# Six written-out turns of GpSimd's gather ring, eighteen more waits behind its drain, and list weights made five chunks at a time

## The chip, the cores and the metric

The kernel runs on one core of a Trainium2 chip. The metric is the device time of a run in microseconds, the median of several runs. The profile covers one execution of the program; its span, from the program's first instruction to its last, is a little shorter than the device time.

## What is computed

For each of eight sequences of 8192 rows of 512 numbers, the reference sums all rows up to the midpoint of the sequence's length, and multiplies the sum by a 512x512 matrix:

```
mask = (pos < lengths[:, None, None]).astype(np.float32)
cs = np.cumsum(x * mask, axis=1)
mid_features = cs[b_idx, lengths // 2, :]
return np.matmul(mid_features[:, None, :], w).squeeze(1)
```

Only rows 0 to `lengths // 2` of each sequence matter, so the kernel reads just those and sums them on TensorE.

## The kernel before

**The pieces of x.** Eight consecutive rows of one sequence make a unit of 16 KB. The first 64 rows of all sequences are always read (`xb`, fetched last, in two parts), so are rows 64 to 255 (`xt`, two early loads), and the rest is a list of units that depends on the lengths. The list is cut into chunks of 128 units, one for each partition; there are at most `C` = 31 chunks, and 13 with this draw of lengths. Each chunk is fetched by one indirect DMA of up to 2 MB into one of `R` = 3 buffers.

**The engines.** Each engine runs its own program, and semaphores tie them together.

- VectorE (line 272 on) works out the list of units (`table`) and the weights, zeros and ones that say which rows of a unit count for which sequence (`weights`, line 355). The weights of the first three chunks are made early; those of chunks 3 to 30 by one call at line 371, after a wait for the first two products. A call is two operations, `early` (a comparison) and `wc` (a product). Each step waits for the one before it. The mark `"w"` stands behind the last.
- GpSimd (line 210 on) issues the gathers: three written out at line 236, and the rest by `ring` (line 123), a loop written out for three turns, one for each buffer, which goes round until a register with the number of chunks left is used up. A turn waits on `s_now`, which ScalarE raises when a chunk's unit numbers are in place. After the last chunk (`gp_end`, line 255) GpSimd issues the two parts of `xb` and the pieces of `w`, drains, and waits for the output stores (`s_out`) before it leaves.
- ScalarE (line 165 on) copies, for each chunk, unit numbers to `now` and weights to `ww`; in the ring's first buffer it waits for the mark `"w"` (line 187).
- SyncE (line 134 on) relays: data landed and weights written gives one count of `s_rdy`.
- TensorE (line 393 on) waits for that count and adds eight products of a chunk to `s_ps`. Between chunks it runs idle products[...]. At the end it adds `xb` into `d_ps`, folds both (`mf_ps`), and multiplies by `w` (`o_ps`), waiting for the pieces of `w` by `s_w`.

SyncE and ScalarE use the same `ring`. All transfers of GpSimd go through one queue in the order of issue, so `xb` and `w` come behind the gathers.

Of the kernel before, what the change touches and what calls it, by code (L numbers as in the profile page):

```python
# [15 lines left out]
def kernel(  # L16
# [22 lines left out]
    R = 3  # L39
# [6 lines left out]
    C = -(-B * (S // 2 // U + 1 - HU) // P)  # L46
    FAR = 1 << 17
    IDLE = 2
    xu = x.rearrange("b (q u) d -> (b q) (u d)", u=U)
    lens_words = lengths.tensor.reshape([B]).bitcast(I32).ap().rearrange("(o t) -> o t", o=1)  # L50

# [8 lines left out]
    def sem(name):  # L60
        return tc.alloc_semaphore(name)
# [45 lines left out]
    s_back = [sem(f"back{k}") for k in range(PARTS)]  # L107
    s_w = [sem(f"w{k}") for k in range(4)]
# [11 lines left out]
    def weights_by_rows(at, n):  # L120
        return ww[:, at * B:(at + n) * B].rearrange("p (u b) -> p u b", b=B)

    def ring(eng, name, left, body):
        for s in range(R):
            with nc.body(f"{name}_0_{s}", valid_engines=[eng.engine]):
                eng.br_cmp(left, s, f"{name}_1_{s}", f"{name}_end", "IS_GT")  # L126
            with nc.body(f"{name}_1_{s}", valid_engines=[eng.engine]):
                body(s)
                if s == R - 1:
                    eng.reg_sub(left, left, R)  # L130
                eng.br(f"{name}_0_{(s + 1) % R}")


    def sync(sp):
        left = sp.alloc_register("left_sp")
        full = sp.alloc_register("full_sp")
        have = sp.alloc_register("have_sp")
        sp.reg_mov(full, 16)
        sp.reg_mov(have, 1)
        sp.wait_ge(s_dve, marks["count"])  # L140
        sp.load(left, count[:])
        sp.wait_ge(s_dve, marks["front"])
        sp.wait_ge(s_zero, 3)
        for f in range(PARTS):
            sp.wait_ge(s_front[f], 16)
            sp.sem_inc(s_rdy, 1)
        sp.br("sy_0_0")

        def relay(s):
            sp.wait_ge(s_wr, have)  # L150
            sp.wait_ge(s_full[s], full)
            sp.sem_inc(s_rdy, 1)
            sp.reg_add(have, have, 1)
            if s == R - 1:
                sp.reg_add(full, full, 16)

        ring(sp, "sy", left, relay)
        with nc.body("sy_end", valid_engines=[sp.engine]):
            sp.wait_ge(s_dve, marks["out0"])
            sp.wait_ge(s_act, 3)  # L160
            store(sp, 0)
            sp.br(END)


    def scalar(act):
# [16 lines left out]
        def weigh(s):  # L182
# [7 lines left out]
            act.reg_add(turn, turn, 1)  # L190

        ring(act, "ac", left, weigh)
        with nc.body("ac_end", valid_engines=[act.engine]):
            act.wait_ge(s_pe, 2)
# [15 lines left out]
    def gpsimd(pool):  # L210
        pool.iota(v_i[:], pattern=[[P * U, C], [1, U]], base=HEAD, channel_multiplier=0)
        pool.iota(r_i[:, FU:], pattern=[[2, BU], [-(BU // 2), FB]], base=0,
                  channel_multiplier=BU // 2).then_inc(s_pool, 1)
        pool.wait_ge(s_pool, 1)
        for k in range(4):
            pool.iota(at_i[32 * k:32 * k + 32], pattern=[[P, C]],
                      base=64 * (k % 2) + 8 * (k // 2) + 63 * 8 * k,
                      channel_multiplier=16).then_inc(s_pool, 1)
        pool.tensor_scalar(out=row[:, 2 * B + 2:], in0=lens[:, ::2], scalar1=0.5, scalar2=0.25,
                           op0=ALU.mult, op1=ALU.add)._wait_ge(s_len, 16).then_inc(s_pool, 1)  # L220
        pool.wait_ge(s_pool, 6)
        pool.iota(r_i[:, :FU], pattern=[[2, FU], [-(FU // 2), FB]], base=2 * TOP,
                  channel_multiplier=FU // 2)
        pool.iota(fold_i[:], pattern=[[-32, 2], [-1, B]], base=P, channel_multiplier=1,
                  ).then_inc(s_pool, 1)

        def fetch(to, units, at, n, full):
            return pool.indirect_dma_start(  # L228
                out=to, out_offset=None, in_=units,
                in_offset=bass.IndirectOffsetOnAxis(ap=at, axis=0),  # L230
                bounds_check=n - 1, oob_is_err=False).then_inc(full, 16)

        left = pool.alloc_register("left_pool")
        pool.wait_ge(s_dve, marks["idx"])
        pool.br("gp_b_0")
        for c in range(R):
            if c > 0:
                with nc.body(f"gp_a_{c}", valid_engines=[pool.engine]):
                    pool.br_cmp(left, c, f"gp_b_{c}", "gp_end", "IS_GT")
            with nc.body(f"gp_b_{c}", valid_engines=[pool.engine]):  # L240
                got = fetch(xt[:, c], xu, now[:, c:c + 1], B * UB, s_full[c])
                if c > 0:
                    got._wait_ge(s_done, c)
                if c == 0:
                    pool.load(left, count[:])  # L245
                if c == R - 1:
                    pool.reg_sub(left, left, R)
                pool.br(f"gp_a_{c + 1}" if c + 1 < R else "gp_0_0")

        def gather(s):  # L250
            fetch(xt[:, s], xu, now[:, s:s + 1], B * UB, s_full[s])._wait_ge(s_now, 1)
            pool.sem_inc(s_now, -1)  # L252

        ring(pool, "gp", left, gather)
        with nc.body("gp_end", valid_engines=[pool.engine]):
            for f in range(PARTS):
                pool.dma_start(out=xb[:, f], in_=x[FB * f:FB * (f + 1), :TOP].rearrange(  # L257
                    "b (q u) d -> q b (u d)", u=BU)).then_inc(s_back[f], 16)
            pool.dma_start(out=wt[:, :2], in_=w[HALVES[0]].rearrange("(p k) d -> p k d", k=2),
                           ).then_inc(s_w[0], 16)  # L260
            pool.dma_start(out=wt[:, 2], in_=w[QUARTERS[2]]).then_inc(s_w[1], 16)
            for g, at in enumerate(HALVES):
                pool.dma_start(out=wt[:, 3, at], in_=w[QUARTERS[3], at]).then_inc(s_w[2 + g], 16)  # L263
            pool.drain()
            pool.wait_ge(s_out, 32)
            pool.br(END)

# [4 lines left out]
    def vector(dve):  # L272
        def step(do, *args, wait=True, **kw):
            if done[0] and wait:
                dve.wait_ge(s_dve, done[0])
            do(*args, **kw).then_inc(s_dve, 1)  # L276
            done[0] += 1
# [4 lines left out]
        def mark(name):  # L282
            marks[name] = done[0]
# [30 lines left out]
        def over(t, a, n):  # L314
            return t.unsqueeze(1).to_broadcast((P, a, n))
# [39 lines left out]
        def weights(a, e):  # L355
            n = e - a
            step(tt, out=early[:, a:e].rearrange("p c u b -> p (c u) b"),
                 in0=v_f[:, a * U:e * U].unsqueeze(2).to_broadcast((P, n * U, B)),
                 in1=over(ends[:], n * U, B), op=ALU.is_lt)
            step(tt, out=wc[:, a:e].rearrange("p c (u b) -> p c u b", b=B), in0=early[:, a:e],  # L360
                 in1=ge[:, a:e, :B].unsqueeze(2).to_broadcast((P, n, U, B)), op=ALU.mult)
# [6 lines left out]
        step(ts, out=fold2[:], in0=fold_m[:], scalar1=0, scalar2=None, op0=ALU.is_equal)  # L368
        step(tt, out=fold[:], in0=fold2[:, 0], in1=fold2[:, 1], op=ALU.add)
        dve.wait_ge(s_done, PARTS)  # L370
        weights(R, C)
        mark("w")
        all_done = dve.alloc_register("all_done_dve")
        dve.load(all_done, count[:])
# [18 lines left out]
    def tensor(pe):  # L393
# [5 lines left out]
        def idle(n):  # L399
            for _ in range(n):  # L400
                pe.matmul(idle_ps[:FB], lhsT=ones[:, :FB], rhs=ones[:, :1].to_broadcast((P, D)),  # L401
                          start=True, stop=True, skip_group_check=True)
# [24 lines left out]
        with nc.body("pe_idle", valid_engines=[pe.engine]):  # L427
            idle(IDLE)
            pe.br("pe_to")
# [4 lines left out]
        with nc.body("pe_end", valid_engines=[pe.engine]):  # L434
# [17 lines left out]
            for k in range(KC):  # L452
# [9 lines left out]
            pe.br(END)  # L462

    programs = [(nc.vector, vector, "dv"), (nc.sync, sync, "sy"), (nc.scalar, scalar, "ac"),
                (nc.gpsimd, gpsimd, "gp")]
    for f in range(PARTS):
        nc.sync.dma_start(out=xt[:, f + 1, :FU * D], in_=x[FB * f:FB * (f + 1), TOP:HEAD].rearrange(
            "b (q u) d -> q b (u d)", u=FU)).then_inc(s_front[f], 16)
    nc.scalar.dma_start(out=lens[:], in_=lens_words).then_inc(s_len, 16)
    left = nc.tensor.alloc_register("left_pe")  # L470
# [37 lines left out]
```

## Time and profile before

| what | value |
|---|---|
| device time, median of 3 runs | 83.02 us (82.86 to 83.16) |
| span of the profiled execution | 80.4 us |
| granted TensorE clock | 0.996 |
| bytes moved by DMA | 31.23 MB, 388 GB/s over the span |
| gathers | 13, 0.98 us each on GpSimd (median) |
| `early` and `wc` for chunks 3 to 30 | 2.0 us each on VectorE |
| GpSimd's drain at line 264 | 11.99 us, from 65.6 us |

The page cuts the span into 40 slices of 2 us and gives for each the busy share of every engine, of the DMA engines, and the bytes moved. Busy time of GpSimd is that of its engine; its waits, branches and the drain belong to its sequencer and are listed apart. "Idle before" names what ended an engine's idle time. A chain of waits, followed back from the last instruction, shows what the end waited for.

### The profile page before, as it was taken

The numbers are of one execution on the slowest core, as the hardware profiler recorded it, in microseconds if no ns is written. First come the engines' busy times: TensorE is split into PE (matmuls) and PEld (weight loads), VectorE is DVE, ScalarE is ACT, GpSimd is POOL, SyncE is SP. The second block draws the span as 40 slices with busy tenths as digits, with TensorE's granted clock in tenths as the row PEclk, the third lists the DMA queues.
The fourth block names the chain that finished last, engine by engine and source line by source line (L and its number), as shares of the span: only waits on it lengthen the run. The fifth ranks groups of instructions, "written<-read, shape, count | busy, mean of one in ns | idle before, by whom it ended". The sixth has DMA issues, their size and how long they took to land.

```text
span 80.4 us, 1176 instructions
## 1 busy us (share of the span) xinstructions
PE 59.6 (74%) x360; PEld 14.1 (18%) x360; DVE 11.8 (15%) x43; ACT 9.7 (12%) x31; POOL 19.9 (25%) x32
## 2 busy tenths in 40 slices
PE   0599998997693957939488493975939679399940
PEld 0212212120110202112020110201102021112820
DVE  0799300891000000000000000000000000003130
ACT  2971010102010010201001020010100100000220
POOL 5432050754022040310404004040220793000000
PEclk9999999999999999999999999999999999999998
DMA  0899999999999999999999999999999999999700
GB/s 0 299 428 434 442 418 432 432 424 448 399 456 416 432 432 432 440 399 448 432 415 448 432 424 416 432 448 399 448 432 424 416 432 448 399 373 409 285 0 8
DMA packets 2803, 31.23 MB, mean 388 GB/s; under 512 B 434, under 2 KB 450, under 8 KB 962
## 3 DMA queue, kind: packets, MB, share of 16 engines
q0 software_dynamic: 2480, 28.05, 82.4%
q1 hardware_dynamic: 304, 3.15, 9.7%
q8 instruction: 1, 0.02, 0.1%
q10 hardware_dynamic: 18, 0.01, 0.0%
HBM read 32.51 MB, written 0.02 MB: 404 GB/s over the span
## 4 chain that ended last, share of the span: by engine, by line
issue 59%; POOL 14%; DMA 14%; PE 5%; DVE 2%; POOLq 2%; ACTq 0%; SPq 0%
POOL xt L228 14%; DMA xb<-in_x_dram 12%; DMA lens<-in_lengths_dram 1%; PE mf_ps L446 1%; PE o_ps L395 1%; PE d_ps L395 1%; PE bc_ps L408 1%; DVE o_sb L276 1%; POOL xb L257 1%; POOLq L245 1%; PE mf_ps L449 1%; POOLq L228 0%; DVE row L276 0%; POOLq L126 0%; DVE ge L276 0%
## 5 line engine op out<-in xcount | busy, mean ns | idle before, releaser
L395 PE MATMUL s_ps<-xt,ww 128*8 128x512 f32 x240 | 29.5, 598 | 14.6 <-PEq L415 14.6
L401 PE MATMUL idle_ps<-ones 128*4 128x512 f32 x58 | 29.6, 637 | 0.0
L228 POOL DMA_INDIRECT xt<-in_x_dram,now x13 | 14.8, 1135 | 45.9 <-POOLq L252 36.7
L395 PEld LDWEIGHTS s_ps<-xt,ww 128*8 128x8 f32 x240 | 5.9, 89 | 37.8 <-issue 37.6
L276 DVE COPY s_sb<-s_ps 128x256 f32<-128x256 f32 x2 | 0.8, 420 | 55.3 <-PE s_ps L395 55.3
L401 PEld LDWEIGHTS idle_ps<-ones 128*4 128x4 f32 x58 | 5.1, 90 | 20.4 <-issue 20.4
L185 ACT COPY now<-idx 128x1 int32 x10 | 1.9, 192 | 44.1 <-PE s_ps L395 44.1
L276 DVE TENSOR_TENSOR early<-v_f,ends 128x192 f32<-128x192 f32 (+1 forms) x2 | 2.4, 1192 | 5.5 <-PE s_ps L395 5.5
L408 PE MATMUL bc_ps<-row,ones 1*128 1x26 f32 x2 | 0.6, 396 | 2.9 <-DVE p L276 2.9
L188 ACT COPY ww<-wc 128x64 f32 x10 | 2.4, 244 | 0.1
L276 DVE TENSOR_TENSOR wc<-early,ge 128x192 f32<-128x192 f32 (+1 forms) x2 | 2.4, 1192 | 0.1
L166 ACT ACTIVATE xt<-xt 128x2048 uint32<-128x2048 uint32 x1 | 1.9, 1910 | 0.0
L196 ACT COPY d_sb<-d_ps 128x128 f32<-128x128 f32 x2 | 0.4, 268 | 12.1 <-PE d_ps L395 12.1
L178 ACT COPY ww<-wc 128x64 f32<-128x64 f32 x3 | 0.7, 244 | 8.2 <-PE s_ps L395 6.8
L166 ACT ACT_TABLE_LOAD x1 | 1.3, 1283 | 1.5 <-SPq L52 1.5
L395 PE MATMUL d_ps<-xb,ww 128*8 128x256 f32 x16 | 1.3, 388 | 0.1
L446 PE MATMUL mf_ps<-fold,s_sb 128*128 128x8 f32 x8 | 1.3, 265 | 0.0
L257 POOL DMA_DIRECT2D xb<-in_x_dram x2 | 1.2, 614 | 0.0
L446 PEld LDWEIGHTS mf_ps<-fold,s_sb 128*128 128x128 f32 x8 | 1.1, 197 | 0.4 <-DVE s_sb L276 0.4
L263 POOL DMA_DIRECT2D wt<-in_w_dram x2 | 1.2, 647 | 0.0
L395 PE MATMUL o_ps<-wt,mf_sb 128*8 128x128 f32 x32 | 1.1, 273 | 0.0
L408 PEld LDWEIGHTS bc_ps<-row,ones 1*128 1x128 f32 x2 | 0.5, 308 | 2.9 <-DVE p L276 2.9
(47 smaller groups left out, 14.1 us busy)
## 6 DMA issues: line engine op xcount, KB each, us to landing
xt<-in_x_dram SPq DMA_DIRECT2D x2, 1536.0 KB, 8.3
xb<-in_x_dram POOLq DMA_DIRECT2D x2, 512.0 KB, 9.4
wt<-in_w_dram POOLq DMA_DIRECT2D x1, 512.0 KB, 10.5
wt<-in_w_dram POOLq DMA_DIRECT2D x1, 256.0 KB, 10.7
wt<-in_w_dram POOLq DMA_DIRECT2D x2, 128.0 KB, 10.4
xt<-in_x_dram,now POOLq DMA_INDIRECT x13, 11.7
lens<-in_lengths_dram ACTq DMA_DIRECT2D x1, 0.1 KB
out_dram<-o_sb SPq DMA_DIRECT2D x1, 8.0 KB
```

The costliest lines, as they stand in the source:

```text
L166: act.memzero(xt[:, 1:, FU * D:]).then_inc(s_zero, 1)
L185: act.copy(out=now[:, s:s + 1], in_=idx[:, bass.ds(c, 1)]).then_inc(s_now, 1)
L188: act.copy(out=weights_of(s), in_=wc[:, bass.ds(c, 1)].rearrange("p c e -> p (c e)"),).then_inc(s_wr, 1)
L228: return pool.indirect_dma_start(out=to, out_offset=None, in_=units, in_offset=bass.IndirectOffsetOnAxis(ap=at, axis=0), bounds_check=n - ...
L245: pool.load(left, count[:])
L257: pool.dma_start(out=xb[:, f], in_=x[FB * f:FB * (f + 1), :TOP].rearrange("b (q u) d -> q b (u d)", u=BU)).then_inc(s_back[f], 16)
L263: pool.dma_start(out=wt[:, 3, at], in_=w[QUARTERS[3], at]).then_inc(s_w[2 + g], 16)
L276: do(*args, **kw).then_inc(s_dve, 1)
L395: return pe.matmul(to[32 * j:32 * j + weights.shape[1], :rows.shape[1]], lhsT=weights, rhs=rows, start=start, stop=False, skip_group_check ...
L401: pe.matmul(idle_ps[:FB], lhsT=ones[:, :FB], rhs=ones[:, :1].to_broadcast((P, D)), start=True, stop=True, skip_group_check=True)
L408: pe.matmul(bc_ps[:, :3 * B + 2], lhsT=ones[:1], rhs=row[:], start=True, stop=True,)._wait_ge(s_dve, marks["row"]).then_inc(s_pe, 1)
L446: pe.matmul(mf_ps[i][:, B * (k % 2):B * (k % 2 + 1)], lhsT=s_sb[:, QUARTERS[k]], rhs=fold[:], start=(k % 2 == 0), stop=False, skip_group_c ...
```

## The change

Three edits. `ring` gets the number of turns that are written out as an argument, and GpSimd's ring is written out for six in place of three; the buffers still go round by three, and SyncE's and ScalarE's rings stay as they are. Behind its drain GpSimd waits for both parts of `xb` and all four semaphores of `w`, and then twelve more times for w's last piece, before it waits for the stores. And VectorE makes the weights of chunks 3 to 30 in six calls, five of five chunks and one of three, in place of one call of 28.

The first two lengthen GpSimd's program and change what it does after its last issue. The third cuts two long operations of VectorE, which run beside GpSimd's gathers, into twelve short ones.

```
+    PAD = 12
-    def ring(eng, name, left, body):
-        for s in range(R):
+    def ring(eng, name, left, body, turns=R):
+        for s in range(turns):
             with nc.body(f"{name}_0_{s}", valid_engines=[eng.engine]):
                 eng.br_cmp(left, s, f"{name}_1_{s}", f"{name}_end", "IS_GT")
             with nc.body(f"{name}_1_{s}", valid_engines=[eng.engine]):
-                body(s)
-                if s == R - 1:
-                    eng.reg_sub(left, left, R)
-                eng.br(f"{name}_0_{(s + 1) % R}")
+                body(s % R)
+                if s == turns - 1:
+                    eng.reg_sub(left, left, turns)
+                eng.br(f"{name}_0_{(s + 1) % turns}")
...
-        ring(pool, "gp", left, gather)
+        ring(pool, "gp", left, gather, 2 * R)
...
             pool.drain()
+            for landed in (*s_back, *s_w):
+                pool.wait_ge(landed, 16)
+            for _ in range(PAD):
+                pool.wait_ge(s_w[3], 16)
             pool.wait_ge(s_out, 32)
...
         dve.wait_ge(s_done, PARTS)
-        weights(R, C)
+        for a in range(R, C, 5):
+            weights(a, min(a + 5, C))
```

## The prediction

> **What bounds the kernel now.** I read the 40 slices first, then the queues, then the windows of two microseconds, then the chain that ended last, and last the single instructions of the edited lines.
>
> ```profile
> DMA  0899999999999999999999999999999999999700
> GB/s 0 299 428 434 442 418 432 432 424 448 399 456 416 432 432 432 440 399 448 432 415 448 432 424 416 432 448 399 448 432 424 416 432 448 399 373 409 285 0 8
> q0 software_dynamic: 2480, 28.05, 82.4%
> q8 instruction: 1, 0.02, 0.1%
> ```
>
> The DMA engines are full from the second slice to the last but four. Every slice between moves about 430 GB/s, so 31.23 MB at that rate are 72.6 us of the 80.4. Nearly all of it is GpSimd's queue. One packet on a queue of its own is no data: it is a fetch of instructions.
>
> ```profile
> 52.00:54.00 2.00, 1.82 (x8) 0.20 (x3) 0.00 (x0) 0.39 (x2) 0.98 (x1) 1.00 1.02 434
> 70.00:72.00 2.00, 2.00 (x20) 0.38 (x16) 0.00 (x0) 0.00 (x0) 0.00 (x0) 1.00 0.92 361
> 74.00:76.00 2.00, 1.91 (x24) 1.42 (x20) 0.59 (x3) 0.43 (x2) 0.00 (x0) 1.00 0.95 359
> 76.00:78.00 2.00, 1.25 (x35) 0.93 (x34) 0.74 (x3) 0.51 (x2) 0.00 (x0) 1.00 0.05 12
> ```
>
> In the windows (PE, PEld, DVE, ACT, POOL busy, clock, DMA share, GB/s) the share of the DMA engines is still 0.95 in 74 to 76 us and 0.05 after it: the stream ends near 76.4 us.
>
> ```profile
> 57.88 0.98 POOL L228 DMA_INDIRECT xt<-in_x_dram,now  x1 [3.91 <-POOLq L252]
> 62.78 0.99 POOL L228 DMA_INDIRECT xt<-in_x_dram,now  x1 [3.91 <-POOLq L252]
> DMA to landing us min/median/max: 8.8/11.7/11.8
> ```
>
> Gathers are issued every 4.90 us and land 11.7 us later, so 2.4 of them are always queued. GpSimd idles 3.91 us in each turn: its ring is far from the limit. That the chain of waits names GpSimd and "issue" for most of the span is only the way back through buffers that come free; what frees them is the stream.
>
> ```profile
> 64.33 9.75 DMA xb<-in_x_dram
> 74.13 0.64 PE d_ps L395 x8
> 76.26 1.00 PE o_ps L395 x32
> 77.59 0.29 DVE o_sb L276
> ```
>
> The tail: `xb` lands at 74.09, TensorE folds and multiplies until 77.25, copies, two stores. By the semaphores' records w's four pieces land at 75.38, 76.08, 76.41 and 76.72, and the stores at 79.29. GpSimd's branch that waits for the stores starts at 79.32, and the closing barriers end at 80.45. The run has 83.02, so 2.57 us lie outside the span.
>
> [...]a packet of 16,384 bytes starts at 76.05 us and takes 1.10 us, while TensorE goes through its last products. TensorE does not stop for it[...]. It also has one packet of 8,192 bytes, 0.44 us, at 82.73 us, 2.28 us behind the span's end[...]. [...]the gather at 14.53 us, beside VectorE's two long products, takes 2.65 us, all later ones 0.98.[...]
>
> **The change part by part.**
>
> *VectorE's later list weights.* Removed: `early` and `wc` of 128x1792, 2.025 and 2.027 us, from 14.29 to 18.38. Added: chunks 3 to 30 in five pieces of 320 elements and one of 192, two operations each. The rows 128x192 (0.358) and 128x1792 (2.025) give (2.025 - 0.358) / 1600 = 1.042 ns an element, so 320 elements cost 0.358 + 128 x 1.042 ns = 0.491. Twelve operations: 2 x (5 x 0.491 + 0.358) = 5.63; eleven steps between them at the 0.03 us seen between the two: 0.33. VectorE ends at 14.29 + 5.96 = 20.25, 1.9 us later. Who waits: ScalarE alone, for the mark "w" in front of its copy of weights at 18.55, which moves to 20.3. Behind that in its queue is the next turn's work, released at 22.8, and the weights themselves are used with the fourth gather, which lands at 30.48. VectorE's own next work is at 73.66. On the path: 0.
>
> *The gathers beside it.* The third gather (14.53 to 17.18) meets short operations with gaps in place of long ones: at best 0.98 us, at worst VectorE's end, 20.25. The fourth at 18.75 now meets VectorE too: 0.98 to 2.65 us. The second gather lands at 20.68, the third at 25.60.[...] I take 1 to 2.7 us for both, hidden behind the queued gathers; the worst would leave the DMA engines dry for about 1 us.
>
> *The ring of six.* Ten turns follow the first three gathers. Two of three register subtractions with their branch go, 2 x 0.14 us, inside 3.91 us of idling per turn. From the count-down of the semaphore to the next gather a turn takes 0.227 us whether the ring wraps (28.300 to 28.527) or not (33.184 to 33.411). On the path: 0. It adds 15 instructions to the program (five a turn).
>
> *The waits behind the drain.* 18 waits: two for `xb`, four for w, twelve more for w's last piece. The drain at line 264 ends at 65.56 + 11.99 = 77.55; w's last piece landed at 76.72, so all are met. Two such instructions in a row on GpSimd start 0.078 us apart (79.678, 79.756): 18 x 0.078 = 1.40, done at 78.95. Queued behind them is only the wait for the stores, met at 79.29: 0.34 us to spare. On the path: 0. The least interval seen on this sequencer is 0.065 (1.17 us in all); were each as long as the 0.176 after a taken branch, they would end at 80.7 and cost 1.4.
>
> *Where GpSimd's program lies.* This is the one thing in which the edits reach outside the stream. The compiled kernel before has 68 instructions for GpSimd, labels left out, and 266 for TensorE. TensorE's fetch at 76.05 lies between its waits for w at 75.40 and 76.21, its 196th and 229th.[...] With 15 + 18 = 33 more, its end is at 101, and the step falls among the waits behind the drain, where GpSimd idles and the DMA engines are free. A fetch would then leave the run's last microseconds. What it costs there no row shows:[...] its packet, 0.44 us; or 1.10, the longest fetch seen. I take 0.5 us.
>
> **Sum for the likeliest case:** 83.02 - 0.5 = 82.5 us.
>
> **The rivals.**
> 1. *No change.* The stream, the tail and the barriers are as before and the fetch was never waited for. For it: every edit has its slack inside the span, and TensorE did not stop at its own fetch. Against it: the 8,192-byte packet stands at the very end of the run, where nothing hides it. 83.0 us.
> 2. *Slower: the fetch falls into the stream.* The step could come with the issues of `xb` and w at 63.8 to 66.5 us, while all DMA engines are full. A 16 KB packet takes 0.61 us on its engine and 8 KB about half, so that engine's share of w lands 0.31 to 0.61 us later, at 77.0 to 77.3. TensorE's last quarter needs 0.49 us after it (76.76 to 77.25), so it ends 0.27 to 0.6 later: 83.3 to 83.6.[...]
> 3. *Slower: a new wait takes its place.* The waits behind the drain outlast the stores (up to 84.4), or the third gather starves the stream (up to 84.0). Against both: slack of 0.34 us at the dearest pair seen, and a gather that got through in 2.65 us even beside two unbroken products.
>
> **How the numbers follow.** Faster by a moved fetch 0.46, spread over 0.3 to 1.1 us. No change 0.33. Fetch in the stream 0.15 and a new wait 0.06, together slower 0.21. The time is the first case's, 82.5. The low end takes a whole fetch of 1.10: 81.9. The high end takes in the no-change case and most of the second rival: 83.5.
>
> **What would show it.** Right: a span within 0.2 us of 80.4, windows of about 430 GB/s up to 76 us, twelve VectorE operations of 0.49 or 0.36 us ending near 20.3, all eighteen waits over before 79.3, and a smaller difference between run and span; an instruction packet at 77.5 to 79 us in place of that at 82.7. Wrong: the run follows the span and the difference stays 2.6 us (no change), an instruction packet in 63 to 76 us with w landing late (second rival), or GpSimd's branch after its waits later than the stores (third). A gain inside the stream, before 76 us, would overturn the reading, since I give none there.

## The result and the profile after

The changed kernel takes 83.65 us (median of 6 runs, 83.50 to 84.15), the kernel before beside it 82.92 us (median of 6): a ratio of 1.0092, 95% interval 1.0063 to 1.0122. It is slower by 0.9%, where 82.5 us and a gain were forecast.

The 40 slices and the queues of the changed kernel:

```profile
DMA  0899999999999999999999999999999999999200
GB/s 0 332 434 416 475 394 434 426 426 402 459 426 410 459 418 418 459 410 434 434 418 394 475 418 402 467 418 418 459 410 434 442 410 418 382 406 408 74 12 0
q0 software_dynamic: 2480, 28.05, 81.4%
q8 instruction: 1, 0.02, 0.1%
q14 instruction: 1, 0.01, 0.0%
```

The stream is the same stream: full from the second slice to the 37th, the same 28.05 MB on GpSimd's queue. New is the last line. A second fetch of instructions, one packet of 8,192 bytes, now lies inside the span.

The chain of waits of the changed kernel, its end:

```profile
64.26 9.76 DMA xb<-in_x_dram
74.06 0.64 PE d_ps L401 x8
76.19 1.00 PE o_ps L401 x32
77.53 0.29 DVE o_sb L281
```

Up to the last copy everything stands within 0.1 us of the kernel before, and a little earlier (77.53 against 77.59). Yet the span is 81.5 us in place of 80.4. So the whole loss, 1.0 us, lies behind that copy, which ends at 77.8 us; from there on no engine computes. Beside it and behind it the timeline has only the two stores, first of the kernel before and then of the changed one:

```profile
77.64 0.37 SPq L207 DMA_DIRECT2D out_dram<-o_sb  x1
77.98 0.55 ACTq L207 DMA_DIRECT2D out_dram<-o_sb  x1
```

```profile
77.57 0.37 SPq L208 DMA_DIRECT2D out_dram<-o_sb  x1
77.91 0.55 ACTq L208 DMA_DIRECT2D out_dram<-o_sb  x1
```

Both are issued 0.07 us earlier than before. What comes after them shows in GpSimd's waits behind the drain (count, durations in ns, first and last start). In the kernel before there is one, the branch that waits for the stores; in the changed kernel lines 269 and 270 hold them:

```profile
L266 POOLq COMPARE_BRANCH  x1: 43/43/43, 79.3 to 79.3; - x1
```

```profile
L269 POOLq EVENT_SEMAPHORE  x8: 42/43/43, 77.5 to 78.5; - x8
...
L270 POOLq EVENT_SEMAPHORE  x1: 43/43/43, 80.3 to 80.3; - x1
```

For the eighteen waits and that for the stores the profile has nine instructions, eight and one, and a branch behind them: two waits share one instruction. The eighteen are over sooner than forecast: eight are done at 78.55. But the wait for the stores, at line 270, ends at 80.25 in place of 79.32. By the semaphores' records the stores have landed at 80.23, not at 79.29.

The records of single packets and instructions in the trace show where the time goes. "Pause" is the start of the last GpSimd instruction ahead of an unusual gap, and of the one behind it; "fetch" is from the start of its packet to its end, and packets of the stores are given by their start; "full" is when the stores' semaphore is complete. Times in us:

```
                GpSimd's        fetch, 8 KB     last packet of   last packet of   stores
                pause           of GpSimd       the 1st store    the 2nd store    full
before          none in span    none in span    78.56            78.90            79.29
after           77.78-78.25     79.07-79.39     78.49            79.39            80.23
```

Between the fourth and fifth of the eight waits, 0.47 us pass on GpSimd's sequencer in place of 0.09, and the fetch follows 0.82 us after the end of this pause; I call it GpSimd's because it follows GpSimd's pause here and in the runs below. I call the place of the pause the step; what makes GpSimd pause there, no run shows. The fetch begins only after GpSimd has gone on (79.07 against 78.25), so it does not bring the instruction that follows the pause; what it brings, no run shows either. Seven of the eight packets of the second store begin by 78.84; the eighth begins at 79.39, in the moment in which the fetch's packet ends (79.39). I read this as the fetch standing in front of it on the same DMA engine. The packet comes 0.55 us behind the seventh, of which the fetch's packet fills the last 0.32; why the hold begins before that packet does, the trace does not show. From the packet's start to the full semaphore it takes 0.84 us where the last one before took 0.40.

Against that the run gained something outside the span: the run's time minus its span is 2.13 us (median of the six) where the kernel before has 2.48 (median of 52 runs in the experiments). Plus 1.0 in the span, minus 0.35 outside it, is 0.65; the medians differ by 0.73.

### The profile page after: what moved, and what is told of

Its sections match the earlier page's. It is cut to its first block, busy times and chain, and to the rows that moved or that the text cites. A ratio compares the mean times of both kernels' runs of the same rounds, so it can differ in the third digit from the quotient of the medians.

```text
span 81.5 us, 1191 instructions
## 1 busy us (share of the span) xinstructions
PE 58.7 (72%) x360; PEld 14.0 (17%) x360; DVE 13.5 (17%) x53; ACT 9.7 (12%) x31; POOL 18.4 (23%) x32
## 3 DMA queue, kind: packets, MB, share of 16 engines
q0 software_dynamic: 2480, 28.05, 81.4%
## 4 chain that ended last, share of the span: by engine, by line
issue 58%; POOL 16%; DMA 12%; PE 5%; POOLq 2%; DVE 1%; SPq 0%
POOL xt L229 14%; DMA xb<-in_x_dram 12%; PE mf_ps L452 1%; PE o_ps L401 1%; PE d_ps L401 1%; PE bc_ps L414 1%; POOL at_i L217 1%; DVE o_sb L281 1%; POOL xb L258 1%; POOLq L246 1%; PE mf_ps L455 1%; POOL v_i L212 1%; POOLq L229 0%; POOLq L127 0%; POOL row L220 0%
## 5 line engine op out<-in xcount | busy, mean ns | idle before, releaser
L401 PE MATMUL s_ps<-xt,ww 128*8 128x512 f32 x240 | 28.9, 593 | 15.3 <-PEq L421 15.3
L407 PE MATMUL idle_ps<-ones 128*4 128x512 f32 x58 | 28.6, 618 | 0.0
L229 POOL DMA_INDIRECT xt<-in_x_dram,now x13 | 13.2, 1017 | 47.4 <-POOLq L253 39.0
L281 DVE TENSOR_TENSOR early<-v_f,ends 128x320 f32<-128x320 f32 (+1 forms) x7 | 3.2, 454 | 4.7 <-PE s_ps L401 4.5
L281 DVE TENSOR_TENSOR wc<-early,ge 128x320 f32<-128x320 f32 (+1 forms) x7 | 3.2, 454 | 0.2
## 6 DMA issues: line engine op xcount, KB each, us to landing
xt<-in_x_dram,now POOLq DMA_INDIRECT x13, 11.7
```

The costliest lines, as they stand in the source:

```text
L229: return pool.indirect_dma_start(out=to, out_offset=None, in_=units, in_offset=bass.IndirectOffsetOnAxis(ap=at, axis=0), bounds_check=n - ...
L401: return pe.matmul(to[32 * j:32 * j + weights.shape[1], :rows.shape[1]], lhsT=weights, rhs=rows, start=start, stop=False, skip_group_check ...
```

## The experiments

Three theories stood against each other. *The fetch*: GpSimd's step now falls close to the stores, and its fetch holds one of their packets. *The waits*: eighteen more instructions of the sequencer are simply too many. *VectorE*: the chunks, or the granted clock (0.979 in this profile, 0.984 to 0.995 in the other five runs, which were no faster), cost the time. All ratios are to the kernel before on the same chip.

**One edit at a time.** e1_ring keeps only the ring of six:

```
-        ring(pool, "gp", left, gather)
+        ring(pool, "gp", left, gather, 2 * R)
```

> Only the ring of six. Fetch theory ([...]in the changed kernel it runs just ahead of the output stores and holds one of their packets): the boundary, at GpSimd's 78th instruction in the changed kernel, now falls into the closing barriers, after the stores. Stores land at 79.3 us as before, the span grows by 0.3 to 0.5 us (the sequencer's pause at the boundary), run minus span falls from 2.5 to about 2.1; time 82.7 to 83.1. Waits theory (the eighteen waits themselves last too long): 82.9, span 80.4. VectorE theory (the chunked weights or the clock cost the time): 82.9, span 80.4.

Measured: 83.15 us, ratio 1.0018 (0.9996 to 1.0039). The median span rises from 80.6 to 81.0, run minus span falls from 2.48 to 2.14. In the profiled execution GpSimd pauses inside the closing barriers (79.84 to 80.30), the fetch comes at 80.99, and the stores are full at 79.47, no packet of them late. That is what the fetch theory expected; only the time lies 0.05 us above its range, and it is not told apart from the kernel before.

e2_waits keeps only the waits:

```
             pool.drain()
+            for landed in (*s_back, *s_w):
+                pool.wait_ge(landed, 16)
+            for _ in range(PAD):
+                pool.wait_ge(s_w[3], 16)
```

> Only the waits behind the drain, ring of three. Fetch theory: GpSimd's program ends at 77 instructions, just ahead of the boundary, so no fetch falls into the span; stores land at 79.3, span 80.4 to 80.5, run minus span 2.4 to 2.6, time 82.8 to 83.0. Waits theory: as slow as the changed kernel, span 81.5, time 83.6. VectorE theory: 82.9.

Measured: 83.34 us, ratio 1.0026 (1.0008 to 1.0044). The waits do not reproduce the loss of 0.7 us. For the eight waits the profile has:

```profile
L269 POOLq EVENT_SEMAPHORE  x8: 43/43/43, 77.7 to 78.4; - x8
...
L270 POOLq EVENT_SEMAPHORE  x1: 43/43/43, 79.5 to 79.5; - x1
```

Without the pause eight take 0.61 us from first to last start, and the wait for the stores ends at 79.5, not 80.3. The fetch theory's expectation missed: I had put GpSimd's end just ahead of its step, and the step still fell into the span, at the semaphores' clearing in the last barrier (80.22 to 80.81 from one instruction to the next, against 0.22 us before). The median span is 81.2 and run minus span 2.15, and a loss of 0.2 us is left that is clear of noise. The profiled execution accounts for the 0.6 us of span: 0.38 of pause, 0.13 by which the drain right behind it takes longer (0.16 against 0.03), and 0.09 for one more wait instruction between the stores' landing and GpSimd's exit.

Counted in the compiled programs, without labels and with each gather once, the pause comes ahead of GpSimd's 69th instruction in both, and in the changed kernel too. The kernel before ends at 62 in this count, closing barriers included (68 in the prediction's, which has each gather twice), and its span shows no such pause.

e3_dve keeps only VectorE's chunks:

```
-        weights(R, C)
+        for a in range(R, C, 5):
+            weights(a, min(a + 5, C))
```

> Only VectorE's chunks. Fetch theory and waits theory: span 80.4, time 82.8 to 83.0, third gather about 1.1 us in place of 2.65; an instruction packet of VectorE may come up near 82 us. VectorE theory: span 81.5, time 83.6.

Measured: 83.05 us, ratio 0.9995 (0.9966 to 1.0025), median span 80.6. The gathers in its timeline:

```profile
14.70 1.12 POOL L229 DMA_INDIRECT xt<-in_x_dram,now  x1 [3.76 <-PE s_ps L397]
18.95 1.07 POOL L229 DMA_INDIRECT xt<-in_x_dram,now  x1 [3.13 <-POOLq L253]
```

The third gather takes 1.12 us in place of 2.65, and the time does not move: it was hidden. The VectorE theory falls; the clock has nothing to explain either, since up to the last copy the changed kernel is not behind.

e4_nodve is the change without VectorE's chunks: the diffs of e1_ring and e2_waits together.

> The change without VectorE's chunks: ring of six and waits. Fetch theory: all of the loss stays, stores land near 80.2 us, an 8,192-byte instruction packet near 79.1, span 81.4 to 81.6, time 83.5 to 83.8. Waits theory: the same time, but GpSimd's waits end after 79.3 us and the stores land at 79.3. VectorE theory: 82.9.

Measured: 83.76 us, ratio 1.0089 (1.0055 to 1.0123). The whole loss is there. The pause is at 77.98 to 78.45, the fetch at 79.26, the second store's last packet at 79.58, the stores full at 80.42. Its waits end in time; what is late is again the wait for the stores:

```profile
L269 POOLq EVENT_SEMAPHORE  x8: 43/43/43, 77.7 to 78.7; - x8
...
L270 POOLq EVENT_SEMAPHORE  x1: 43/43/43, 80.4 to 80.4; - x1
```

Neither edit alone makes it, both together do, where one alone gives 0.0 and 0.2 us: they add up in instructions, not in time. The waits theory falls.

**Moving the step.** If the fetch costs only where it meets the stores, moving the step must move the loss. None of the next five has VectorE's chunks.

e5_late: ring of three, and

```
+    PAD = 30
...
             pool.drain()
+            for landed in (*s_back, *s_w):
+                pool.wait_ge(landed, 16)
+            for _ in range(PAD):
+                pool.wait_ge(s_w[3], 16)
```

> Ring of three, 36 waits behind the drain (18 instructions), no VectorE chunks: the step[...] falls behind the sixteenth of them, near 79.0 us, after both stores were handed to the DMA engines. Fetch theory: the pause of 0.38 us ends near 79.4, no store packet is held, the stores land at 79.3 to 79.4, span 80.5 to 80.7, run minus span 2.1, time 0.2 to 0.4 us below the kernel before. Rival (any fetch inside the span costs what it cost in the changed kernel, wherever it lies): span 81.5, 0.6 us above. Rival (the waits are the cost): twice as many waits, slower than the changed kernel.

Measured: 82.97 us, ratio 0.9989 (0.9976 to 1.0002). There are twice the waits, and no loss.

```profile
L269 POOLq EVENT_SEMAPHORE  x17: 42/43/43, 77.7 to 79.5; - x17
...
L270 POOLq EVENT_SEMAPHORE  x1: 43/43/43, 79.6 to 79.6; - x1
```

The pause is at 79.04 to 79.50, the stores are full at 79.46, and no packet is late; the median span is 80.8 (up 0.2) and run minus span 2.14. The expected gain of 0.2 to 0.4 us came out as 0.1, and not clear of noise: the pause ends a little behind the stores and delays GpSimd's exit.

e6_mid: as e5_late with PAD = 24, and four more instructions ahead of the last issues, where GpSimd has time. They hold eight met waits, that is, waits for something that came long ago:

```
         with nc.body("gp_end", valid_engines=[pool.engine]):
+            for _ in range(8):
+                pool.wait_ge(s_len, 16)
```

> Ring of three, eight met waits (four instructions) ahead of the last issues, 30 waits (15 instructions with that for the stores) behind the drain: the step falls behind the twelfth, near 78.7 us, its pause ends near 79.1, inside the wait for the stores. Fetch theory: stores land at 79.3 unless the fetch still reaches their engine first, span 80.4 to 80.6, run minus span 2.1, time 0.3 to 0.4 us below the kernel before. Rival (any fetch in the span costs): span 81.5, 0.6 us above.

Measured: 82.84 us against 83.12, ratio 0.9970 (0.9952 to 0.9987). This one is faster than both kernels. The pause is at 78.56 to 79.03, while the stores are still on their way, and they are full at 79.31.

```profile
L271 POOLq EVENT_SEMAPHORE  x14: 43/43/43, 77.6 to 79.1; - x14
...
L272 POOLq EVENT_SEMAPHORE  x1: 43/43/43, 79.3 to 79.3; - x1
```

The wait for the stores (line 272 here) ends at 79.3 as in the kernel before, although the fetch lies in the span. Its median span is up by 0.1 us, run minus span down from 2.51 to 2.13.

e7_ring9: ring of nine, no waits.

```
-        ring(pool, "gp", left, gather)
+        ring(pool, "gp", left, gather, 3 * R)
```

> Ring of nine, no waits, no VectorE chunks: the step falls at the ninth turn, near 58 us, in the middle of the stream. Fetch theory: nothing meets the stores; 8 KB more on one of the full DMA engines puts w's last landing back by up to 0.3 us, run minus span 2.1, time between 0.4 below and level with the kernel before. Rival (the second case of the prediction, the fetch in the stream is the dear one): 0.3 to 0.6 us above.

Measured: 82.99 us, ratio 0.9992 (0.9980 to 1.0005). The step comes at the ninth turn (pause 57.99 to 58.43); the fetch's packet begins only at 62.15, while the DMA engines are full (their share is 1.02 in 62 to 64 us). The median span is up by 0.2, and run minus span is 2.16. So a fetch in the middle of the stream costs the span about 0.2 us at most; the 0.3 to 0.6 us of the prediction's second rival look too dear, though a step among the last issues, where the rival had it, was not tried.

e8_first: e4_nodve with the eight met waits ahead of the last issues, as in e6_mid.

> The change without VectorE's chunks, and with eight met waits (four instructions) ahead of the last issues: the step falls at the first wait behind the drain, near 77.6 us, 0.35 us earlier than in the changed kernel. Fetch theory: the fetch is 0.35 us earlier, so it holds the second store's packet 0.2 us or not at all, or the first store's instead; stores land at 79.3 to 80.0, span 80.4 to 81.2, time from 0.4 below to 0.4 above the kernel before. Rival (any fetch in the span costs the same): span 81.5, 0.6 us above.

Measured: 83.69 us, ratio 1.0063 (1.0040 to 1.0086). The step falls between the drain's end and the first wait: 0.42 us pass there (78.20 to 78.62), where e4_nodve has 0.04.

```profile
L271 POOLq EVENT_SEMAPHORE  x8: 43/43/43, 78.6 to 79.2; - x8
...
L272 POOLq EVENT_SEMAPHORE  x1: 43/43/43, 80.7 to 80.7; - x1
```

In the profiled execution the fetch's packet lasts from 79.30 to 79.84, and now a packet of the *first* store is held, until 79.83 where the other seven began by 79.24, and one of the second behind it, until 79.88. The stores are full at 80.70. The packet that is held changed with the time of the step. That profile is the longest of its six runs, so its times are to be compared with one another only.

e9_eight: as e6_mid with sixteen waits ahead of the last issues and PAD = 16.

> As e6_mid, with sixteen met waits (eight instructions) ahead of the last issues and four instructions fewer behind the drain: the step falls behind the eighth wait, near 78.3 us, four instructions later than in the changed kernel and four earlier than in e6_mid. In e4_nodve the step came at 78.0, the fetch's packet began at 79.26 and the packets of the first store (78.6) still went ahead of it. Fetch theory: with 0.35 us more, the second store's packets (78.8 to 79.0) go ahead too; stores land at 79.3 to 79.4, span 80.5 to 80.7, time 0.2 to 0.4 us below the kernel before. If the fetch still comes first, the stores land near 80.4 and the time is 0.6 above.

Measured: 82.87 us, ratio 0.9976 (0.9957 to 0.9994). The pause is at 78.62 to 79.09, and no packet is late.

```profile
L271 POOLq EVENT_SEMAPHORE  x10: 42/43/43, 78.0 to 79.2; - x10
...
L272 POOLq EVENT_SEMAPHORE  x1: 43/43/43, 79.8 to 79.8; - x1
```

The pause ends 0.66 us behind the start of the second store's issue (78.43). In the changed kernel and in e4_nodve it ended 0.34 and 0.35 behind it, and a packet was held; in e8_first it ended 0.29 behind that of the first store, and a packet of that one was held. In these profiled executions the limit lies between 0.35 and 0.66 us.

One thing these runs leave mixed. The three slow kernels have both the ring of six and the waits, and none of the others has both: no run puts a later step into a kernel with both edits. That the place of the step decides, and not the two edits in some other way, rests on the packets: in all three slow kernels the held packet begins within 4 ns of the end of the fetch's (79.389 and 79.393, 79.584 and 79.588, 79.835 and 79.838).

**The best of both.** e10_mid_dve is e6_mid with VectorE's chunks.

> e6_mid with VectorE's chunks as in the change. If the chunks are off the path, as e3_dve has it: the same as e6_mid, 0.1 to 0.4 us below the kernel before, third gather 1.1 us. If VectorE's longer program costs in the closing part[...]: 0.2 us or more above e6_mid.

Measured: 82.76 us against 83.12, ratio 0.9953 (0.9935 to 0.9972), the fastest of the study. It is not told apart from e6_mid, whose interval overlaps. e3_dve had run minus span at 2.37, 0.11 below the kernel before, which would fit a step of VectorE's own that now comes sooner. The traces point the same way: the three kernels with the chunks have one more fetch of 8,192 bytes, 0.64 to 0.67 us behind their spans (at 82.11 us in the changed kernel, 81.35 and 81.43 in e3_dve and e10_mid_dve), and no other kernel has one there. Whose fetch it is, no run shows, and what it costs was not tried by itself.

## Why the prediction was wrong

**The bound, the stream and the edits inside it: right.** The stream ended as before (w's last piece at 76.64 against 76.72). VectorE's twelve operations were forecast at 0.491 and 0.358 us. The changed kernel's timeline has:

```profile
13.53 0.49 DVE L281 TENSOR_TENSOR early<-v_f,ends 128x320 f32<-128x320 f32 x1 [4.53 <-PE s_ps L401]
14.05 0.49 DVE L281 TENSOR_TENSOR wc<-early,ge 128x320 f32<-128x320 f32 x1
...
19.18 0.36 DVE L281 TENSOR_TENSOR wc<-early,ge 128x192 f32<-128x192 f32 x1
```

They end 6.01 us after their start (forecast 5.96). The third gather, 1.12 us, lies at the low end of its range, and e3_dve shows the chunks and the shorter gather to be worth nothing. The ring's turns were off the path, as e1_ring shows.

**The waits: off the path as forecast, off in count.** Two share one instruction. They are done by 78.55 (forecast 78.95), and e5_late has twice as many without loss.

**The moved fetch: right in place, and the gain a little small.** The step does fall among the waits: in the prediction's count, with each of the nine written-out gathers twice, it comes ahead of the 78th instruction. That it would lie behind the end of the kernel before and ahead of the end of the changed one was my estimate, which no trace of the kernel before shows. Run minus span fell by 0.35 us (2.48 to 2.13) where 0.5 was taken. (The prediction's 2.57 set the median time against the span of one execution; that execution's own difference is 2.47.) In every kernel whose step of GpSimd lies in the span it is 2.10 to 2.17; in those whose step does not, 2.37 to 2.52. In size this is the sequencer's pause: from one instruction to the next 0.47 us in place of 0.09, that is 0.38 us. TensorE went on with its products (76.26 to 77.26 in the kernel before) while a packet of 16,384 bytes was fetched (76.05 to 77.15); that a fetch would cost GpSimd's sequencer as little does not hold.

**The step that failed** is the one that put the fetch "among the waits behind the drain, where GpSimd idles and the DMA engines are free". They are not: the two output stores go out from 78.4 to 78.9 us, and they are what the end waits for. The sum had no term for it. It measures 0.93 us on the stores' landing (79.29 to 80.23): the last packet begins 0.49 us later than before, and it takes 0.44 us more until the semaphore is full. Another 0.09 us is the one more wait instruction between the landing and the end (1.24 us in place of 1.15). Minus the 0.35 gained, that leaves 0.67 us; the medians differ by 0.73, and the spans of the six runs scatter from 81.4 to 82.0.

**The rivals.** The second had the right idea, a fetch in front of data on a DMA engine, at the wrong place: it thought only of w's pieces in the full stream, and a fetch earlier in that stream cost about 0.2 us at most (e7_ring9). My reading, which no run tests by itself: the stream, with about 2.4 gathers queued at any time (landing 11.7 us after issue, one every 4.90 us), has slack for one late engine, and a store of eight packets for which the end waits has none (0.93 us on its landing). The third asked whether the waits outlast the stores, and not what they set off.

**What stays open.** Why the semaphore is full 0.84 us behind the held packet's start in place of 0.40 no run tells apart; e4_nodve and e8_first have 0.84 and 0.82 too. That fetch and packet were on one DMA engine is read from their times in the three slow kernels and from the change of the held packet in e8_first; the trace does not name the engine of a packet.

## What to carry to other kernels

Here added instructions moved GpSimd's pause and an 8 KB fetch into the span, to 77.78 and 79.07 us in the changed kernel, and did so although they cost next to nothing themselves (thirty-six waits in e5_late: ratio 0.9989). After such an edit, look where the fetch's packet lies and what else is on the DMA engines then. The small store at the very end had no slack: one packet late by 0.49 us, and it landed 0.93 us later. It was enough that the pause ended 0.66 us or more behind the store's issue, inside the wait for the stores: that gained 0.3% (e6_mid) where a pause ending 0.35 us behind it lost 0.9% (e4_nodve and the changed kernel). When two edits cost little each (ratios 1.0018 and 1.0026) but much together (1.0089), count instructions as well as microseconds.

## What the runs showed of the hardware

- GpSimd's sequencer rested 0.38 us more at one place in its program, with no branch there: from one instruction to the next 0.47 against 0.09 us between waits (changed kernel), 0.46 against 0.08 in the closing barriers (e1_ring).
- The pause came ahead of the same instruction, the 69th in the compiled program, in the changed kernel and in e1_ring, e2_waits, e4_nodve, e5_late, e6_mid, e7_ring9, e8_first, e9_eight and e10_mid_dve, whatever that instruction was.
- The 8 KB fetch began 0.7 to 0.9 us behind the end of the pause where the stream was over, and 3.7 us behind it in the full stream (e7_ring9).
- In the changed kernel one packet of 1 KB that began at the end of a fetch's, 0.49 us later than in the kernel before, went with a delay of 0.93 us of the semaphore that waits for it.
